# The low halves of the GLU's weights: VectorE behind the last scan in place of GpSimd, nine parts loaded ahead, and the GLU begun on high halves

## The chip, the cores and the metric

The kernel runs on one core of one Trainium2 chip. The metric is the time of one execution in device microseconds (us). Three executions of the kernel before gave 2034.98, 2035.56 and 2037.89 us; the median is 2035.56 us. One further execution was recorded by the hardware profiler; all times of single instructions come from it, counted from the start of its span.

## The reference: what is computed

One layer of an encoder: an S5 state-space mixer with a gated linear unit (GLU), then a convolutional feed-forward network (FFN), over 2048 tokens of width 1024 and 16 tokens put ahead of them. Cut to what matters here:

```
u  = (rms_norm(h) @ w_in).reshape(b, L, 64 groups, 16)
s  = associative scan over time of  s[t] = a * s[t-1] + B u[t]     (complex, 64 states a group)
y  = gelu(Re(C s) + d * u)                                         (b, L, 1024)
a, g = split(y @ w_glu, 2)                                         (w_glu is 1024 x 2048)
h  = h + a * sigmoid(g)
h  = h + conv_ffn(rms_norm(h))
```

## The kernel before

**Products in halves.** Every large matrix product is made of float16 halves. A float32 operand is scaled, rounded to float16 (the high half), and what rounding lost is kept as a second float16 (the low half). A product is the sum of three matmuls: high by high, high by low, low by high. For the GLU the weights' halves are `wg[0]` (high) and `wg[1]` (low), the activations' halves are the two planes of `yT`.

**The S5 stage.** The 1024 channels are worked in eight blocks of 128 (`p` or `cb`, 0 to 7). For each block there are: the input product (`emit_u`), tables made by VectorE (`gen_b`, `gen_c`, the latter giving `CA`), a small kernel matrix (`emit_k`, written to DRAM as `kd` and read back in Toeplitz form by `load_toep` as `Toep`), the states' inputs (`emit_v`, giving `S`), a scan in place on VectorE (`scan`, thirty short instructions on `S`, lines 547 to 552), a rearrangement of the scanned states by DMA (`emit_z`: `Z` from `S`), and the output (`emit_y`): 32 tiny matmuls `mp`, then for each of the block's eight groups two matmuls of `U` by `Toep` (L598, L599) and one of `Z` by `CA` (L600); ScalarE's GELU (L602) takes two groups at a time into `yf`, and one DMA (L606) writes `yf` to DRAM as `yd`. In the text y5, y6, y7 and Z6, Z7 and so on are these steps of blocks 5, 6 and 7.

**The GLU's operands.** The weights come in 16 parts (`split_wg`, part i holds rows 128*(i//2) of the weight and one half of its 2048 columns): GpSimd issues the load of 512 KB into a staging tile `gst` (L96); then the part is split. In the kernel before, parts 0 to 7 are split by two ScalarE operations (L102 scales in place, L103 rounds to `wg[0]`) and one of GpSimd (L104 subtracts, giving `wg[1]`); parts 8 to 15 by two of VectorE (L99, L100). As a part is split, the next one's load is issued. The activations come in 16 tiles of 128 tokens: `load_y` reads columns of `yd` (SyncE, L113), `prep_y` makes the halves `yh` (L123 or L125 the high one, L126 the low one), and SyncE issues two transposing DMAs (L128) into `yT`. A tile may be taken in pieces: columns of blocks 0 to 4, 5 and 6, 7 for tile 0; 0 to 6 and 7 for tile 1. A tile needs 8 (blocks) x 3 (half products) x 4 (quarters of the columns) = 96 matmuls (`glu_mm`, L137); tiles 0 and 1 together 192.

**Order.** Every engine and queue runs its instructions in the order in which the program lists them; nothing is rescheduled (`manual_schedule`). A DMA is listed on the queue of the engine that issues it, and that queue stands still while its next instruction waits. The last two blocks are written out by hand at the end of the S5 stage. Block 6's pass (`pen`) interleaves its scan with block 7's tables and the first `prep_y` of tile 0; then, outside the loop, come `gen_c(7)`, `emit_k(7)`, the scan of block 7, `emit_y(6)`, `emit_z(7)`, the first GLU matmuls of tile 0, the loads of tile 1 and of blocks 5 and 6 of tile 0, `emit_y(7)`, and the rest. After that only TensorE's work is left for the GLU: the remaining matmuls of tiles 0 and 1, tiles 2 to 15, and then the FFN.

Of the kernel before, what the change touches and what calls it, by code (L numbers as in the profile page):

```python
# [44 lines left out]
def tile_kernel(ctx: ExitStack, tc: tile.TileContext, x, meta, norm_mix, norm_ffn, w_in, lam_re, lam_im, log_dt,  # L45
# [45 lines left out]
    def split_wg(i, pool, tag, bufs):  # L91

        dk, hh = divmod(i, 2)
        cs_ = slice(D * hh, D * hh + D)
        st = pool.tile([P, D], F32, tag=tag, bufs=bufs, name=f"gst{dk}_{hh}")
        PO.dma_start(out=st, in_=w_glu[0, dk * P:(dk + 1) * P, cs_])  # L96
        yield
        if wg_eng[0] is V:
            V.tensor_scalar(wg[0][:, dk, cs_], st, GS, None, op0=ALU.mult)  # L99
            V.scalar_tensor_tensor(wg[1][:, dk, cs_], st, GS, wg[0][:, dk, cs_], op0=ALU.mult, op1=ALU.subtract)  # L100
        else:
            A.activation(st, st, AF.Copy, scale=GS)  # L102
            A.copy(wg[0][:, dk, cs_], st)  # L103
            PO.tensor_tensor(wg[1][:, dk, cs_], st, wg[0][:, dk, cs_], op=ALU.subtract)  # L104
# [10 lines left out]
    def prep_y(t, tile_of, d0=0, d1=DK, eng=A):  # L115

        w = P * (d1 - d0)
        if t not in yT:
            yT[t] = gl.tile([P, 2, DK, P], F16, tag="yT", bufs=2, name=f"yT_{t}")
        yt = yts.pop(t)  # L120
        yh = [tile_of("yh", [P, D], F16, f"yh{t}_{d0}_{i}") for i in range(2)]
        if eng is A:
            A.activation(yh[0][:, 0:w], yt[:, 0:w], AF.Copy, scale=YS)  # L123
        else:
            V.tensor_scalar(yh[0][:, 0:w], yt[:, 0:w], YS, None, op0=ALU.mult)  # L125
        V.scalar_tensor_tensor(yh[1][:, 0:w], yt[:, 0:w], YS, yh[0][:, 0:w], op0=ALU.mult, op1=ALU.subtract)  # L126
        for i in range(2):
            SY.dma_start_transpose(out=yT[t][:, i, d0:d1], in_=yh[i][:, 0:w])  # L128

    def glu_mm(t, d0=0, d1=DK):  # L130
        if t not in gps:
            tags = ("u", "u", "v", "v") if t % 2 == 0 else ("t", "t", "y", "y")
            gps[t] = [psum.tile([P, 512], F32, tag=tags[i], name=f"g{t}_{i}") for i in range(4)]
        for dk in range(d0, d1):
            for (a, b) in ((0, 0), (0, 1), (1, 0)):
                for o in range(4):
                    PE.matmul(out=gps[t][o], lhsT=yT[t][:, a, dk], rhs=wg[b][:, dk, 512 * o:512 * o + 512],  # L137
                              start=(dk == 0 and a + b == 0), stop=(dk == DK - 1 and a == 1))


    with ExitStack() as c2:
# [437 lines left out]
        def emit_y(cb, mid=None):  # L579
# [14 lines left out]
            for gp in range(4):  # L594
# [8 lines left out]
                             yp.rearrange("p g (t h) -> p g t h", h=T), AF.Gelu_apprx_tanh)  # L603
                if mid:
                    mid(gp)
            PO.dma_start(out=yd[0:T, :, cb * P:(cb + 1) * P].rearrange("t k c -> k t c"),  # L606
                         in_=yf.rearrange("p t g h -> p t (g h)"))

        def drive(*gens):
            gens = list(gens)  # L610
# [99 lines left out]
            return s5.tile(shape, dt, tag=tag, bufs=bufs, name=nm)  # L710

        def wg_load(i):
            wgs.append(split_wg(i, *((s5, "wit", 2) if i in (6, 7, 11, 12) else (ld, "win", 3))))
            next(wgs[i])

        def wg_split(i0, i1, eng=PO):
            for i in range(i0, i1):
                wg_eng[0] = eng
                next(wgs[i], 0)
                if len(wgs) < 16:  # L720
                    wg_load(len(wgs))

        for p in range(NCB - 1):
            take = quads[:takes[p]]
# [3 lines left out]
            def uq(i, dks=range(DK)):  # L728
                if i < len(take):
                    emit_u(*take[i], dks=dks)  # L730
                    if DK - 1 in dks:
                        evict_u(*take[i])
# [58 lines left out]

    hc2 = ctx.enter_context(tc.tile_pool(name="hc2", bufs=1, side="right"))
# [661 lines left out]
```

## Time and profile before

| | |
|---|---|
| median of three executions | 2035.56 us |
| the profiled execution, its own time | 2040.73 us |
| its span, first to last instruction | 2038.9 us |
| TensorE busy over the span, instructions | 1923.3 us (94%), 10992 |
| VectorE busy | 1384.9 us (68%) |
| ScalarE busy | 645.2 us (32%) |
| GpSimd busy | 577.2 us (28%) |
| mean granted TensorE clock | 0.979 |

A row of the timeline gives start, duration (both us), engine, line, operation, output and inputs by the program's names, shapes and count; in square brackets stands how long the engine was idle just before it and what ended that. PE is TensorE, DVE is VectorE, ACT is ScalarE, POOL is GpSimd, SP is SyncE; a `q` behind the name is the engine's queue as it issues DMAs. A row of the windows gives a stretch of the span, its length, each engine's busy time with the number of its instructions in brackets, the clock granted to TensorE (1.00 is full speed), the DMA engines' busy share and what they moved in GB/s. In rows about one tile, three durations are minimum/median/maximum in ns.

### The profile page before, as it was taken

How to read it: one execution, taken by the hardware profiler on the slowest of the kernel's cores; microseconds unless marked ns; L12 is line 12 of the kernel's file. 1: busy time of each engine (PE TensorE's matmuls, PEld its weight loads, DVE VectorE, ACT ScalarE, POOL GpSimd, SP SyncE). 2: the span in 40 equal slices, each digit the busy share in tenths (PEclk: the TensorE clock that was granted, in tenths of full speed). 3: DMA queues.
4: the chain of work that ended last, by engine and by line, in shares of the span. 5: the costliest groups of instructions: out<-in, count | busy, mean ns of one | idle time of the engine just before them, and what ended most of it. 6: DMA issues, size and time to landing. Idle time of an engine off the chain costs nothing.

```text
span 2038.9 us, 28973 instructions
## 1 busy us (share of the span) xinstructions
PE 1923.3 (94%) x10992; PEld 957.5 (47%) x10992; DVE 1384.9 (68%) x1709; ACT 645.2 (32%) x1057; POOL 577.2 (28%) x644
## 2 busy tenths in 40 slices
PE   3699999689999999999999989999999999999999
PEld 3456666445444444444444434334444444444444
DVE  3489999944444348999999961345466666668982
ACT  5433423312222224544445441222222232322110
POOL 4221212400000014555555500366000001117630
PEclk9799999789999999999999999999999999999999
DMA  9967766958566656444444489999533333336443
GB/s 187 188 136 140 176 138 150 229 139 185 130 140 158 147 150 178 143 156 148 146 157 148 151 243 274 310 324 303 171 104 101 102 104 101 101 99 156 144 124 93
DMA packets 337223, 329.92 MB, mean 162 GB/s; under 512 B 150700, under 2 KB 238332, under 8 KB 337084
## 3 DMA queue, kind: packets, MB, share of 16 engines
q1 hardware_dynamic: 319164, 286.01, 52.9%
q0 software_dynamic: 8496, 27.30, 4.7%
q10 hardware_dynamic: 9424, 14.76, 2.9%
q8 instruction: 86, 1.41, 0.3%
q14 instruction: 53, 0.43, 0.1%
HBM read 183.82 MB, written 108.45 MB: 143 GB/s over the span
## 4 chain that ended last, share of the span: by engine, by line
PE 66%; DVE 8%; DMA 4%; issue 2%; ACT 1%; POOL 1%; SPq 1%; DVEq 0%; ACTq 0%; POOLq 0%
PE g L137 15%; PE p L78 11%; PE p L76 11%; PE p L77 11%; PE pq L76 3%; PE pq L77 3%; PE pq L78 3%; PE po L76 2%; PE po L77 2%; PE po L78 2%; DMA wc<-wcd 1%; DMA wcd<-wc 1%; DVE wc L914 1%; DVE y L1132 1%; DVE y L1131 1%
## 5 line engine op out<-in xcount | busy, mean ns | idle before, releaser
L76 PE MATMUL p<-hc,wc 128*128 128x512 f16 x1232 | 467.3, 379 | 2.3 <-DMA hc<-hl 1.7
L78 PE MATMUL p<-hc,wc 128*128 128x512 f16 x1232 | 467.5, 379 | 1.7 <-DVE wc L914 1.7
L77 PE MATMUL p<-hc,wc 128*128 128x512 f16 x1232 | 467.4, 379 | 0.9 <-DMA hc<-hl 0.9
L137 PE MATMUL g<-wg,yT 128*128 128x512 f16 x1536 | 334.3, 381 | 0.7 <-DMA yT<-yh 0.7
L914 DVE SCALAR_TENSOR_TENSOR wc<-fst,wc 128x512 f16<-128x512 f32 x209 | 184.7, 892 | 109.9 <-ACT wc L908 91.4
L137 PEld LDWEIGHTS <-yT 128*128 128x128 f16 x1536 | 150.2, 98 | 183.1 <-issue 2.6
L908 ACT ACTIVATE wc<-fst 128x512 f16<-128x512 f32 x209 | 125.9, 625 | 229.6 <-POOL fst L873 97.5
L78 PEld LDWEIGHTS <-wc 128*128 128x128 f16 x1232 | 120.2, 98 | 148.7 <-DVE wc L914 3.8
L76 PEld LDWEIGHTS <-wc 128*128 128x128 f16 x1232 | 120.1, 98 | 140.0 <-issue 1.8
L77 PEld LDWEIGHTS <-wc 128*128 128x128 f16 x1232 | 120.2, 98 | 138.9 <-DMA hc<-hl 1.2
L76 PE MATMUL pq<-wc,act 128*128 128x512 f16 x352 | 135.2, 384 | 16.6 <-DMA wc<-wcd 11.1
L76 PE MATMUL u<-hnT,win 128*128 128x512 f16 (+2 forms) x352 | 115.2, 337 | 25.6 <-DMA hnT<-hl 14.8
L77 PE MATMUL pq<-wc,act 128*128 128x512 f16 x352 | 135.1, 384 | 0.0
L78 PE MATMUL pq<-wc,act 128*128 128x512 f16 x352 | 134.8, 383 | 0.0
L77 PE MATMUL u<-hnT,win 128*128 128x512 f16 (+2 forms) x352 | 114.9, 337 | 16.9 <-DMA hnT<-hl 16.9
L76 PE MATMUL po<-wc,act 128*128 128x512 f16 x308 | 117.6, 382 | 3.4 <-DVE res L1292 3.4
L77 PE MATMUL po<-wc,act 128*128 128x512 f16 x308 | 117.6, 382 | 0.0
L78 PE MATMUL po<-wc,act 128*128 128x512 f16 x308 | 117.4, 381 | 0.0
L78 PE MATMUL u<-hnT,win 128*128 128x512 f16 (+2 forms) x352 | 115.0, 337 | 0.0
L1123 ACT ACTIVATE act<-hu,cwt 128x1024 f32<-128x1024 f32 x44 | 54.6, 1241 | 185.6 <-DVE hu L1224 141.3
L77 PEld LDWEIGHTS <-act 128*128 128x128 f16 x660 | 64.8, 98 | 99.1 <-issue 23.3
L1123 ACT ACTIVATE y<-hu,cwt 128x1024 f32<-128x1024 f32 x44 | 54.6, 1240 | 162.3 <-DVE hu L1224 123.2
(328 smaller groups left out, 2983.6 us busy)
## 6 DMA issues: line engine op xcount, KB each, us to landing
wc<-wcd SPq DMA_DIRECT2D x275, 256.0 KB, 2.7
wcd<-wc SPq DMA_DIRECT2D x253, 256.0 KB, 3.2
fst<-in_ffn_w_up_dram SPq DMA_DIRECT2D x44, 512.0 KB, 5.1
fst<-in_ffn_w_down_dram SPq DMA_DIRECT2D x44, 512.0 KB, 5.8
ud<-us SPq DMA_DIRECT2D x32, 258.0 KB, 5.3
U<-ud SPq DMA_DIRECT2D x16, 516.0 KB, 3.5
Toep<-kd SPq DMA_DIRECT2D x64, 128.0 KB, 5.4
yd<-yf POOLq DMA_DIRECT2D x8, 1024.0 KB, 7.6
```

The costliest lines, as they stand in the source:

```text
L76: PE.matmul(out=ps, lhsT=sh, rhs=mh, start=first, stop=False)
L77: PE.matmul(out=ps, lhsT=sh, rhs=ml, start=False, stop=False)
L78: PE.matmul(out=ps, lhsT=sl, rhs=mh, start=False, stop=last)
L137: PE.matmul(out=gps[t][o], lhsT=yT[t][:, a, dk], rhs=wg[b][:, dk, 512 * o:512 * o + 512], start=(dk == 0 and a + b == 0), stop=(dk == DK - ...
L908: A.activation(w[:, 0], src, AF.Copy, scale=GS)
L914: V.scalar_tensor_tensor(w[:, 1], src, GS, w[:, 0], op0=ALU.mult, op1=ALU.subtract)
L1123: A.activation(y, hu[:, 2:18], AF.Identity, bias=cwt[:, 3, c:c + 1], scale=cwt[:, 2, c:c + 1])
L1131: V.scalar_tensor_tensor(y, hu[:, 1:17], cwt[:, 1, c:c + 1], y, op0=ALU.mult, op1=ALU.add)
L1132: V.scalar_tensor_tensor(y, hu[:, 0:16], cwt[:, 0, c:c + 1], y, op0=ALU.mult, op1=ALU.add)
```

## The change

What it does, by steps:

- GpSimd's subtraction (L104) and VectorE's pair (L99, L100) are gone. All 16 parts take the same way: ScalarE scales in place and rounds (`wg_hi`), and VectorE makes the low half by one TENSOR_TENSOR (`wg_lo`, L101 of the changed file).
- All 16 of these VectorE operations stand behind the last instruction of block 7's scan. No low half is made before.
- Nine parts have a staging place of their own ahead of any low half. Parts 0 to 2 are loaded as before; 3 to 5 behind `transp(7)`; 6 to 8 behind `gen_c(7)`, into the places of tables that nobody reads any more. Part i + 9 is loaded when part i's low half is made.
- The high half of tile 0's pieces and of tile 1's first piece (`prep_y`) is made by ScalarE in place of VectorE; VectorE still makes the low one.
- The GLU of tile 0 begins with the products that need the weights' high halves alone: blocks 0 and 1 ahead of `emit_k(7)`, blocks 2 and 3 behind `emit_y(6)`. Their products with the low halves (`los`) stand directly ahead of `emit_y(7)`. The kernel before had done 12 + 24 = 36 GLU matmuls ahead of `emit_y(7)`, the changed one has 48 there.
- `emit_z(7)` stands behind `load_y` of tile 1 and of blocks 5 and 6 of tile 0; before, it stood ahead of them.
- The DMAs that write `yd` of blocks 6 and 7 are issued by SyncE in place of GpSimd.

```diff
-        if wg_eng[0] is V:
-            V.tensor_scalar(wg[0][:, dk, cs_], st, GS, None, op0=ALU.mult)
-            V.scalar_tensor_tensor(wg[1][:, dk, cs_], st, GS, wg[0][:, dk, cs_], op0=ALU.mult, op1=ALU.subtract)
-        else:
-            A.activation(st, st, AF.Copy, scale=GS)
-            A.copy(wg[0][:, dk, cs_], st)
-            PO.tensor_tensor(wg[1][:, dk, cs_], st, wg[0][:, dk, cs_], op=ALU.subtract)
+        A.activation(st, st, AF.Copy, scale=GS)
+        A.copy(wg[0][:, dk, cs_], st)
+        yield
+        V.tensor_tensor(wg[1][:, dk, cs_], st, wg[0][:, dk, cs_], op=ALU.subtract)
+        yield
...
-            for (a, b) in ((0, 0), (0, 1), (1, 0)):
+            for (a, b) in of:
...
-            PO.dma_start(out=yd[0:T, :, cb * P:(cb + 1) * P].rearrange("t k c -> k t c"),
-                         in_=yf.rearrange("p t g h -> p t (g h)"))
+            (PO if cb < NCB - 2 else SY).dma_start(out=yd[0:T, :, cb * P:(cb + 1) * P].rearrange("t k c -> k t c"),
+                                                   in_=yf.rearrange("p t g h -> p t (g h)"))
...
+            slots = [(ld, "win", 3)] * 3 + [(s5, "wit", 2)] * 2 + [(ld, "wst", 1), (s5, "tmp", 1), (s5, "pre", 1), (s5, "pim", 1)]
+            wgs.append(split_wg(i, *slots[i % 9]))
...
+        def wg_lo(i0, i1):
+            for i in range(i0, i1):
+                next(wgs[i])
+                if i + 9 < 2 * DK:
+                    wg_load(i + 9)
...
-                fills.append(prep_y(0, s5_tile, 0, NY[0], V) for _ in range(1))
+                fills.append(prep_y(0, s5_tile, 0, NY[0]) for _ in range(1))
...
         p = NCB - 1
-        wg_split(3, 4)
-        wg_load(7)
-        wg_load(8)
+        his, los = ((0, 0), (1, 0)), ((0, 1),)
+        wg_hi(3, 6)
         drive(gen_c(p))
-        glu_mm(0, 0, 1)
+        for i in range(6, 9):
+            wg_load(i)
+        glu_mm(0, 0, 2, his)
         emit_k(p)
         load_toep(p)
-        wg_split(4, 6)
         drive(scan(p))
-        emit_y(p - 1, lambda gp: wg_split(6 + gp, 7 + gp - gp // 2))
-        emit_z(p)
-        glu_mm(0, 1, 3)
+        emit_y(p - 1)
+        wg_hi(6, 8)
+        glu_mm(0, 2, 4, his)
         load_y(1, s5_tile, 0, NY[1])
         load_y(0, s5_tile, NY[0], NY[1])
-        wg_split(8, 12, V)
-        emit_y(p)
-        glu_mm(0, 3, NY[0])
-        prep_y(1, s5_tile, 0, NY[1], V)
-        prep_y(0, s5_tile, NY[0], NY[1], V)
-        wg_split(12, 16, V)
+        emit_z(p)
+        wg_lo(0, 2)
+        prep_y(0, s5_tile, NY[0], NY[1])
+        prep_y(1, s5_tile, 0, NY[1])
+        wg_lo(2, 8)
+        wg_hi(8, 9)
+        glu_mm(0, 0, 4, los)
+        emit_y(p, lambda gp: wg_hi(9 + gp, 10 + gp))
+        wg_lo(8, 13)
+        glu_mm(0, 4, NY[0])
+        wg_hi(13, 16)
+        wg_lo(13, 16)
```

Where instructions move, at three places. In the rows below stand line, operation, output and inputs with the program's numbers, and shape. (The changed file's lines are two less than before's in this part.)

SyncE's queue around Z7, in the kernel before (`kd1` and `Toep7` are block 7's kernel matrix, `yt1_0` the columns of blocks 0 to 6 of tile 1, `yt0_5` those of blocks 5 and 6 of tile 0):

```order
L515 DMA kd1_106<-ks7_3798 32x1x256 x4
L522 DMA Toep7_3804<-kd1_106 16x8x256 x8
L575 DMA Z7_3927<-S7_3710 64x4x128 x4
L113 DMA yt1_0_3956<-yd_69 128x896
L113 DMA yt0_5_3958<-yd_69 128x256
```

The same place in the changed kernel (`yf6` is y6's result, `yh0_5` the halves of `yt0_5`):

```order
L513 DMA kd1_106<-ks7_3802 32x1x256 x4
L520 DMA Toep7_3808<-kd1_106 16x8x256 x8
L604 DMA yd_69<-yf6_3877 128x16x128
L111 DMA yt1_0_3931<-yd_69 128x896
L111 DMA yt0_5_3933<-yd_69 128x256
L573 DMA Z7_3935<-S7_3707 64x4x128 x4
L126 DMA_TRANSPOSE yT_0_3600<-yh0_5_0_3946 128x2x128
```

The store of y6 has come onto this queue, and Z7 has moved from ahead of the two loads to behind them; the loads read what that store writes.

VectorE behind the last instruction of block 7's scan, in the kernel before (`gst4_0` and `gst4_1` are parts 8 and 9):

```order
L552 TENSOR_TENSOR S7_3710<-S7_3710,stab7d0_3859 128x8x63
L99 TENSOR_SCALAR wg0_3489<-gst4_0_3754 128x1024
L100 SCALAR_TENSOR_TENSOR wg1_3490<-gst4_0_3754,wg0_3489 128x1024
L99 TENSOR_SCALAR wg0_3489<-gst4_1_3816 128x1024
L100 SCALAR_TENSOR_TENSOR wg1_3490<-gst4_1_3816,wg0_3489 128x1024
```

The same place in the changed kernel (`gst0_0`, `gst0_1`, `gst1_0`, `gst1_1` are parts 0 to 3):

```order
L550 TENSOR_TENSOR S7_3707<-S7_3707,stab7d0_3853 128x8x63
L101 TENSOR_TENSOR wg1_3490<-gst0_0_3491,wg0_3489 128x1024
L101 TENSOR_TENSOR wg1_3490<-gst0_1_3493,wg0_3489 128x1024
L124 SCALAR_TENSOR_TENSOR yh0_5_1_3947<-yt0_5_3933,yh0_5_0_3946 128x256
L124 SCALAR_TENSOR_TENSOR yh1_0_1_3954<-yt1_0_3931,yh1_0_0_3953 128x896
L101 TENSOR_TENSOR wg1_3490<-gst1_0_3495,wg0_3489 128x1024
L101 TENSOR_TENSOR wg1_3490<-gst1_1_3701,wg0_3489 128x1024
```

Two low halves come first, then the low halves of the two activation pieces, then the other low halves of the weights.

VectorE in block 6's scan, where the first piece of tile 0 is split, in the kernel before:

```order
L547 TENSOR_TENSOR stab6k0_3607<-S6_3398,asc_101 128x16x15
L125 TENSOR_SCALAR yh0_0_0_3610<-yt0_0_3497 128x640
L126 SCALAR_TENSOR_TENSOR yh0_0_1_3611<-yt0_0_3497,yh0_0_0_3610 128x640
L550 TENSOR_TENSOR S6_3398<-S6_3398,stab6k0_3607 128x8x15
L552 TENSOR_TENSOR S6_3398<-S6_3398,stab6k0_3607 128x8x15
```

The same place in the changed kernel:

```order
L545 TENSOR_TENSOR stab6k0_3598<-S6_3398,asc_101 128x16x15
L124 SCALAR_TENSOR_TENSOR yh0_0_1_3602<-yt0_0_3497,yh0_0_0_3601 128x640
L548 TENSOR_TENSOR S6_3398<-S6_3398,stab6k0_3598 128x8x15
L550 TENSOR_TENSOR S6_3398<-S6_3398,stab6k0_3598 128x8x15
L545 TENSOR_TENSOR stab6k1_3609<-S6_3398,asc_101 128x16x14
```

The high half `yh0_0_0` is no longer made here: it has gone to ScalarE, behind the four GELUs of y5 and the high halves of parts 0 to 2, and VectorE's low half, with the rest of block 6's scan behind it, reads it.

More of the change, by code (lines that the diff above doesn't have):

```diff
@@ L85, in tile_kernel @@
     gl = cl.enter_context(tc.tile_pool(name="gl", bufs=1))
-    wg, yT, gps, wg_eng = [], {}, {}, [PO]
+    wg, yT, gps = [], {}, {}
     def alloc_wg():
@@ L128, in prep_y, with glu_mm @@
             SY.dma_start_transpose(out=yT[t][:, i, d0:d1], in_=yh[i][:, 0:w])
-    def glu_mm(t, d0=0, d1=DK):
+    def glu_mm(t, d0=0, d1=DK, of=((0, 0), (0, 1), (1, 0))):
         if t not in gps:
@@ L183, in tile_kernel @@
         NG = NCB * G
-        pre = s5.tile([P, NG, T + 1], F32, name="pre")
-        pim = s5.tile([P, NG, T + 1], F32, name="pim")
+        pre = s5.tile([P, NG, T + 1], F32, tag="pre", name="pre")
+        pim = s5.tile([P, NG, T + 1], F32, tag="pim", name="pim")
         coef = s5.tile([P, NCB, 4, G], F32, name="coef")
@@ L712, in wg_load, with wg_hi @@
         def wg_load(i):
-            wgs.append(split_wg(i, *((s5, "wit", 2) if i in (6, 7, 11, 12) else (ld, "win", 3))))
+            slots = [(ld, "win", 3)] * 3 + [(s5, "wit", 2)] * 2 + [(ld, "wst", 1), (s5, "tmp", 1), (s5, "pre", 1), (s5, "pim", 1)]
+            wgs.append(split_wg(i, *slots[i % 9]))
             next(wgs[i])
-        def wg_split(i0, i1, eng=PO):
+        def wg_hi(i0, i1):
             for i in range(i0, i1):
[L718 to L721, printed above, removed]
+                next(wgs[i])
+        def wg_lo(i0, i1):
+            for i in range(i0, i1):
+                next(wgs[i])
+                if i + 9 < 2 * DK:
+                    wg_load(i + 9)
         for p in range(NCB - 1):
@@ L745, in tile_kernel @@
             if p:
-                emit_y(p - 1, (lambda gp: wg_split(gp, gp + (gp < 3))) if pen else None)
+                emit_y(p - 1, (lambda gp: wg_hi(gp, min(3, gp + 1))) if pen else None)
             if pen:
-                fills.append(prep_y(0, s5_tile, 0, NY[0], V) for _ in range(1))
+                fills.append(prep_y(0, s5_tile, 0, NY[0]) for _ in range(1))
             fills = itertools.chain(*fills)
@@ L762, in tile_kernel @@
             transp(p + 1)
+            if pen:
+                for i in range(3, 6):
+                    wg_load(i)
             uq(2, range(0, 4))
@@ L769, in tile_kernel @@
         p = NCB - 1
-        wg_split(3, 4)
-        wg_load(7)
-        wg_load(8)
+        his, los = ((0, 0), (1, 0)), ((0, 1),)
+        wg_hi(3, 6)
         drive(gen_c(p))
-        glu_mm(0, 0, 1)
+        for i in range(6, 9):
+            wg_load(i)
+        glu_mm(0, 0, 2, his)
         emit_k(p)
         load_toep(p)
-        wg_split(4, 6)
         drive(scan(p))
-        emit_y(p - 1, lambda gp: wg_split(6 + gp, 7 + gp - gp // 2))
-        emit_z(p)
-        glu_mm(0, 1, 3)
+        emit_y(p - 1)
+        wg_hi(6, 8)
+        glu_mm(0, 2, 4, his)
         load_y(1, s5_tile, 0, NY[1])
         load_y(0, s5_tile, NY[0], NY[1])
-        wg_split(8, 12, V)
-        emit_y(p)
-        glu_mm(0, 3, NY[0])
-        prep_y(1, s5_tile, 0, NY[1], V)
-        prep_y(0, s5_tile, NY[0], NY[1], V)
-        wg_split(12, 16, V)
+        emit_z(p)
[10 more added lines that the diff above has]
+        wg_lo(13, 16)
     hc2 = ctx.enter_context(tc.tile_pool(name="hc2", bufs=1, side="right"))
```

## The prediction

> **What bounds the kernel now.** I read the page first, then the windows, TensorE's timeline, and those of VectorE, ScalarE and SyncE. The windows show the only stretch after the start where TensorE is starved, the end of the S5 stage:
>
> ```profile
> 370.00:380.00 10.00, 3.13 (x26) 1.36 (x23) 9.86 (x9) 1.91 (x2) 3.67 (x4) 0.72 1.04 238
> 400.00:410.00 10.00, 4.08 (x49) 2.13 (x47) 9.48 (x17) 0.17 (x1) 0.50 (x1) 0.93 0.71 220
> 430.00:440.00 10.00, 10.00 (x48) 4.57 (x47) 0.56 (x2) 0.31 (x1) 1.58 (x3) 1.00 0.70 205
> ```
>
> TensorE is busy 3.13 and 4.08 of 10 us there while VectorE is busy 9.86 and 9.48; from 430 on TensorE is full at clock 1.00. TensorE's waits in that stretch:
>
> ```profile
> 382.19 1.08 PE L504 MATMUL kp<-CA,bb 128*32 128x256 f32 x8 [2.48 <-DVE CA L493]
> 384.65 0.61 PE L588 MATMUL mp<-U,Toep 128*32 128x1 f32 x32 [1.30 <-DMA Toep<-kd]
> 387.25 1.19 PE L600 MATMUL yp<-CA,Z 128*128 128x256 f32 x2 [0.41 <-DMA Z<-S]
> 397.45 5.34 PE L137 MATMUL g<-wg,yT 128*128 128x512 f16 x24
> 412.26 1.22 PE L600 MATMUL yp<-CA,Z 128*128 128x256 f32 x2 [7.93 <-DMA Z<-S]
> 424.38 33.83 PE L137 MATMUL g<-wg,yT 128*128 128x512 f16 x156
> 458.92 41.61 PE L137 MATMUL g<-wg,yT 128*128 128x512 f16 x192 [0.71 <-DMA yT<-yh]
> ```
>
> From 424.38 TensorE runs without a hole to the end of tiles 0 and 1 (156 matmuls in 33.83 us, 0.217 each), and tile 2 begins at 458.92. What follows is TensorE's own work, which the change leaves alone. So what the change is worth is read at one point: when does y7 end, and how many of the 192 matmuls are then left. Before that stands Z7, which waits for block 7's scan, and VectorE is that scan's engine:
>
> ```profile
> 353.92 2.38 DVE L125 TENSOR_SCALAR yh<-yt 128x640 f16<-128x640 f32 x1
> 357.23 2.70 DVE L550 TENSOR_TENSOR S<-S,stab6k 128x120 f32<-128x120 f32 x1
> 360.38 2.68 DVE L547 TENSOR_TENSOR stab6k<-S,asc 128x224 f32<-128x224 f32 x1
> 372.08 2.60 DVE L552 TENSOR_TENSOR S<-S,stab6d 128x504 f32<-128x504 f32 x1
> 385.89 0.63 DVE L550 TENSOR_TENSOR S<-S,stab7u 128x256 f32<-128x256 f32 x1
> 386.56 2.37 DVE L552 TENSOR_TENSOR S<-S,stab7u 128x256 f32<-128x256 f32 x1
> 388.96 2.91 DVE L547 TENSOR_TENSOR stab7u<-S,asc 128x256 f32<-128x256 f32 x1
> 392.76 0.59 DVE L547 TENSOR_TENSOR stab7k<-S,asc 128x240 f32<-128x240 f32 x1
> 393.39 2.29 DVE L550 TENSOR_TENSOR S<-S,stab7k 128x120 f32<-128x120 f32 x1
> 395.71 0.38 DVE L552 TENSOR_TENSOR S<-S,stab7k 128x120 f32<-128x120 f32 x1
> 396.12 2.68 DVE L547 TENSOR_TENSOR stab7k<-S,asc 128x224 f32<-128x224 f32 x1
> 407.69 0.69 DVE L552 TENSOR_TENSOR S<-S,stab7d 128x504 f32<-128x504 f32 x1
> L104 POOL TENSOR_TENSOR wg<-gst,wg x8: 2113/2140/2577, 353.4 to 396.3; 128x1024 f16<-128x1024 f32 x8
> ```
>
> Instructions of one size take 0.38 or 2.29, 0.59 or 2.68, 0.69 or 2.60 us. There are eight long ones, and eight GpSimd subtractions of 2.14 us.
>
> **Removing GpSimd's subtractions.** With the short rows as measure, the scan of block 6 loses 2.70-0.38, 2.68-0.59 and 2.60-0.69, together 6.3 us; the scan of block 7 loses 2.37-0.63, 2.91-0.63, 2.29-0.38 and 2.68-0.59, together 8.0. The eighth, at 353.92, goes with its instruction. I take all of it as won.
>
> **The high half on ScalarE.** Part of it is given back at once. VectorE reaches the low half of tile 0's first piece at 353.92, and must now wait for ScalarE, whose y5 work is queued ahead:
>
> ```profile
> 358.24 0.59 ACT L602 ACTIVATE yf<-yp 128x512 f32<-128x512 f32 x1
> L123 ACT ACTIVATE yh<-yt x16: 309/1052/1057, 434.1 to 704.8; 128x1024 f16<-128x1024 f32 x14, 128x128 f16<-128x128 f32 x2
> 357.66 2.92 SPq L128 DMA_TRANSPOSE yT<-yh x2
> ```
>
> The last GELU ends at 358.8; a 640-wide rounding lies between 0.31 (128) and 1.05 (1024), some 0.7; so the low half starts near 359.6 and the scan goes on at 360.3 instead of 357.23: 3.1 us late. Net, block 6's scan and `gen_c(7)` end 3.2 us early, and the kernel matrix of block 7 is done near 380 (382.19+1.2-3.2). Block 7's scan ends 3.2+8.0 = 11.2 us early: 408.4-11.2 = 397.2. On SyncE the first transposition can start at 359.5, the second 1.46 later, so the pair ends at 362.4 instead of 360.6: `kd` of block 6, `Toep6` and Z6, queued behind it, are issued 1.8 us later.
>
> **y6.** It ran from Z6's arrival at 387.25 to 397.45, 10.2 us. Its matrix `kp` is ready earlier, but it waited for `Toep6` and Z6 last, which are now issued 1.8 us later; against that, three weight loads that went out beside them come after `gen_c(7)`. Bounds: 1.8 us later, if the transfers take as long as before; 4 us earlier, if only `kp` held it back and both arrive by 383. I leave it where it was, nearest to the rows that show it waiting for DMA twice.
>
> **The SyncE queue.** This is the term that decides. Ahead of Z7 now stand y6's store and two loads that read what it writes:
>
> ```profile
> 397.65 0.60 ACT L602 ACTIVATE yf<-yp 128x512 f32<-128x512 f32 x1 [1.23 <-PE yp L600]
> DMA to landing us min/median/max: 8.8/8.8/8.8
> DMA to landing us min/median/max: 6.1/7.6/9.8
> 408.44 2.66 SPq L575 DMA_DIRECT2D Z<-S  x4
> 411.19 1.03 SPq L113 DMA_DIRECT2D yt<-yd  x2
> 416.85 0.63 DVE L125 TENSOR_SCALAR yh<-yt 128x896 f16<-128x896 f32 x1 [1.03 <-DMA yt<-yd]
> yt<-yd SPq DMA_DIRECT2D x2, 64.0 KB, 1.9
> ```
>
> y6's last GELU ends at 398.25. The store (8.8 us for that of y6, the first landing row; 6.1 to 9.8 over all eight, the second) lands at 407.1 when issued at 398.3; the loads are issued by 408.1; Z7 goes out then, against 408.44 before. So the scan's 11.2 us do not reach Z7. The store goes from GpSimd's queue to SyncE's, which no row shows for it; I take y6's own 8.8, and 6.1 and 9.8 as ends. The second load lands 1.9 us (64 KB) to 5.6 us (416.85 less 411.19, behind a full DMA) after issue; I take 2.5 for its 128 KB. Call that landing M: 410.6, with ends from 403 (early y6, quick store and load) to 417.
>
> The Trainium skill, "DMA: Bandwidth & Descriptors", section "Anatomy of one DMA — SWDGE (gpsimd) path", fits a transfer as 2.0 us plus its bytes over 436 GB/s: an estimate of 4.4 us for this 1 MB. No landing of `yd` in this trace comes under 6.1; by the page the sum below would be 4.4 us smaller, still a loss.
>
> **VectorE behind M.** Two low halves are made by 399.5 and then VectorE stands, with the other fourteen queued, until the tile pieces come:
>
> ```profile
> 409.01 1.23 DVE L100 SCALAR_TENSOR_TENSOR wg<-gst,wg 128x1024 f16<-128x1024 f32 x1
> 417.51 6.23 SPq L128 DMA_TRANSPOSE yT<-yh x4
> 417.52 1.09 DVE L126 SCALAR_TENSOR_TENSOR yh<-yt,yh 128x896 f16<-128x896 f32 x1
> 421.95 0.43 DVE L126 SCALAR_TENSOR_TENSOR yh<-yt,yh 128x256 f16<-128x256 f32 x1 [0.69 <-DMA yT<-yh]
> ```
>
> There are two `yh` buffers, so the second piece waits until the first's transposes have landed. In order: ScalarE's half 0.4, then the first transposition at M+0.5, the second 1.25 later at M+1.75, landing 3.1 after its start as at 421.95 (second issue about 418.8): M+4.9; the 896-wide low half, 1.09: M+6.0; six low halves of parts 2 to 7 at about 1.15 (rows of 1.23, overlapping): M+12.9. Only then can TensorE finish `los`, which stand ahead of y7: y7 starts at M+13.5.
>
> **y7.** TensorE has then been nearly idle since about 402, and y5 shows what a start after idling costs:
>
> ```profile
> 346.29 0.70 PE L598 MATMUL yp<-Toep,U 128*128 128x256 f32 x2
> 350.43 0.65 PE L598 MATMUL yp<-Toep,U 128*128 128x256 f32 x2
> 352.66 0.59 PE L598 MATMUL yp<-Toep,U 128*128 128x256 f32 x2
> ```
>
> Two groups take 4.14 us at first, the next two 2.23. Eight groups at 1.1 and 0.4 for `mp` make 9.2, and the slow start 1.9: y7 ends at M+24.6. By the Trainium skill, "TensorE: Matmul & The Clock Gate", section "What's actually happening", some 3.4 us pass at half rate after an idle window, an estimate of 1.7 us lost in place of 1.9; the trace bears it out, and the sum would be 0.2 smaller.
>
> **Behind y7.** 144 matmuls are left (192-48), 31.2 us. ScalarE makes parts 9 to 15 between and behind y7's GELUs, two operations each of about the 1.05 of the L123 row; part 13 comes just as block 6 of tile 0 wants it, and I charge 1.0 us. Tiles 0 and 1 end at M+56.8 = 467.4, before at 458.2: 9.2 us lost. The wait of 0.71 ahead of tile 2 stays, since `yT` has two places and TensorE frees the one it needs.
>
> **The rest.** The new staging places, loads 3 to 8 and the high halves of parts 0 to 8 cost nothing, as ScalarE idles through 400 to 410 (0.17 busy); without that cover each part would cost 2.1.
>
> **The sum.** +9.2 on the profiled execution, whose own 2040.73 is 5.2 above the median of 2035.56. I put the difference on the median, a little less because a quicker execution has quicker transfers: 2044.5.
>
> **The rivals.**
> *The scan's gain comes through (faster).* If the store and the two loads land before the scan's end, VectorE never waits, and y7 starts at 399.5+13.5. That is M at 399.5, 11.1 earlier: 1.9 us gained, 3.8 with a warm clock. It decides at a store issued before 388; for it speaks that VectorE alone bounded the old stretch, against it that y6 did not even begin before 384.65 and waited on DMA then. A gain over 4.1 us would need y6 some 12 us earlier as well: 0.07, mostly for a dependency that I have read wrong.
> *Transfers land quickly (no measurable change).* y6 2 us early, the store in 6.1, the load in 1.9: M 405.3, 5.3 earlier, +3.9; at the lowest ends of all, about +1.7. The DMA engines are fuller before (1.04 at 370 to 380) than they will be with loads 6 to 8 moved back. 0.20.
> *The tail of the weights also stalls (slower still).* Parts 11 to 15 are loaded only as low halves 2 to 6 are made, all behind M; if they land late, or the last piece of tiles 0 and 1 comes after TensorE wants it, 2 to 5 us are added: +11 to +14. 0.15.
> *The long VectorE instructions are not GpSimd's doing.* Then the scan ends at 405.2, still ahead of M: nothing changes in the sum.
>
> **Chances.** The forecast itself has 0.58. Plus or minus 0.2%, 4.1 us, is about what a measurement of this kernel can tell from no change. Faster 0.07, same 0.20, slower 0.73 (0.58+0.15). The range takes M from 402.5 to 415, which is +1 to +13.5: 2036 to 2049.
>
> **What would show it.** Right: no VectorE instruction of either scan over 1.4 us; VectorE idle about 5.5 us ahead of the low half of tile 0's first piece, waiting for ScalarE; scan 7 ending near 397; Z7 issued near 408, behind a SyncE wait for the store; a VectorE wait of about 10 us behind the second low half; y7 starting near 424 and ending near 435. Wrong: Z7 issued right behind the scan, or y7 starting before 415.

## The result and the profile after

The changed kernel takes 2045.39 us, the median of 11 executions (2041.33 to 2052.45); the kernel before, run beside it, 2035.56 us. The ratio is 1.0058 with a 95% interval of 1.0043 to 1.0074, which is 8.8 to 15.1 us, 11.8 in the middle. The forecast of 9 us lost lies in that interval, near its lower end; the way there was wrong in its first half, ahead of y6, and mostly right in its second.

The profiled execution has a span of 2048.3 us, 9.4 more than before. That difference has three parts. Up to the end of y5 this execution was 7.6 us earlier: y5's last GELU ends at 351.24 in place of 358.83, out of the first 100 us, in which TensorE's waits for the input differ (it is busy for 56.3 us of them in this execution, 48.9 before). Between the end of y5 and the start of tile 2 it lost 12.8 us, and behind tile 2, 4.2 us. So below the stretch from the end of y5's last GELU to the start of tile 2 is the measure, in three pieces. ScalarE's last GELU of y5, of y6 and of y7 in the changed kernel:

```profile
350.65 0.59 ACT L600 ACTIVATE yf<-yp 128x512 f32<-128x512 f32 x1
...
397.08 0.60 ACT L600 ACTIVATE yf<-yp 128x512 f32<-128x512 f32 x1 [1.58 <-PE yp L598]
...
432.65 0.59 ACT L600 ACTIVATE yf<-yp 128x512 f32<-128x512 f32 x1
```

Together with TensorE's rows of the same stretch:

```profile
385.37 0.61 PE L586 MATMUL mp<-U,Toep 128*32 128x1 f32 x32 [13.49 <-DMA Z<-S]
...
416.04 5.36 PE L135 MATMUL g<-wg,yT 128*128 128x512 f16 x10 [11.94 <-DVE wg L101]
...
422.24 0.43 PE L586 MATMUL mp<-U,Toep 128*32 128x1 f32 x32
...
464.12 41.61 PE L135 MATMUL g<-wg,yT 128*128 128x512 f16 x192 [0.75 <-DMA yT<-yh]
```

TensorE now stands for 13.49 us ahead of y6, for the transfers `Toep6` and Z6, and 11.94 us ahead of `los`, for VectorE's low halves; y7 begins right behind `los`. From the end of y5 to the end of y6 are 46.4 us (39.4 before), from there to the end of y7 35.6 (26.9 before), from there to tile 2 30.9 (33.7 before, when 12 more matmuls were left).

VectorE's rows are of the kind that the prediction said they would be:

```profile
351.95 0.83 DVE L124 SCALAR_TENSOR_TENSOR yh<-yt,yh 128x640 f16<-128x640 f32 x1 [5.25 <-issue]
...
389.10 2.35 DVE L101 TENSOR_TENSOR wg<-gst,wg 128x1024 f16<-128x1024 f32 x2
410.04 0.43 DVE L124 SCALAR_TENSOR_TENSOR yh<-yt,yh 128x256 f16<-128x256 f32 x1 [18.59 <-ACT yh L121]
413.76 1.09 DVE L124 SCALAR_TENSOR_TENSOR yh<-yt,yh 128x896 f16<-128x896 f32 x1 [3.30 <-DMA yT<-yh]
414.77 8.03 DVE L101 TENSOR_TENSOR wg<-gst,wg 128x1024 f16<-128x1024 f32 x7
```

The scan ends at 389.1 and two low halves are made; then VectorE stands idle for 18.59 us with the other low halves queued behind a tile piece that has not been loaded. SyncE's queue shows why y6, and with it that piece, came late:

```profile
355.07 4.73 SPq L513 DMA_DIRECT2D kd<-ks  x4
369.33 5.81 SPq L520 DMA_DIRECT2D Toep<-kd  x8
375.27 6.55 SPq L573 DMA_DIRECT2D Z<-S  x4
...
397.70 0.40 SPq L604 DMA_DIRECT2D yd<-yf  x1
405.25 0.80 SPq L111 DMA_DIRECT2D yt<-yd  x2
406.16 2.72 SPq L573 DMA_DIRECT2D Z<-S  x4
```

And of its waits, those for `kd` (total in us, times, longest; the longest is the one for `kd6`):

```profile
SPq L520 <- DMA kd<-ks: 10.8, 3, 9.4
```

`kd6` is issued by 359.8, and `Toep6`, which reads it, only at 369.33: SyncE waited 9.4 us at a stretch for it to land. The same two rows of the kernel before, where that wait was 6.3 us:

```profile
360.68 2.73 SPq L515 DMA_DIRECT2D kd<-ks  x4
369.86 5.51 SPq L522 DMA_DIRECT2D Toep<-kd  x8
```

Counted from the end of y5, `Toep6` goes out 18.1 us behind it in place of 11.0. Of these 7.1 us, 2.0 lie ahead of `kd6` (its first issue comes 3.8 us behind y5 in place of 1.9, behind the transposes that wait for ScalarE's high half), 2.0 in its four issues (4.73 us in place of 2.73) and 3.1 in the wait for its landing. What else was on its way, GpSimd's queue tells; first that of the kernel before, then of the changed one:

```profile
363.01 0.56 POOL L96 DMA_DIRECT2D gst<-in_s_w_glu_dram  x1 [0.30 <-POOL wg L104]
363.57 1.19 POOL L606 DMA_DIRECT2D yd<-yf  x1
```

```profile
352.25 1.18 POOL L604 DMA_DIRECT2D yd<-yf  x1 [16.11 <-ACT cs L473]
353.79 0.54 POOL L96 DMA_DIRECT2D gst<-in_s_w_glu_dram  x1 [0.36 <-PE wt L463]
355.12 1.06 POOL L96 DMA_DIRECT2D gst<-in_s_w_glu_dram  x2 [0.79 <-PE wt L463]
```

Before, GpSimd's subtractions held its queue, and y5's store of 1 MB went out at 363.57, 4.7 us behind y5's end and behind `kd6` (issued 360.68 to 363.4). Freed of them, GpSimd sends it 1.0 us behind y5's end, and three weight loads of 512 KB with it, all ahead of or beside `kd6`. Three such loads went out around `kd6` in the kernel before, too, at 356.96, 360.00 and 363.01, spaced by the subtractions; the store ahead of `kd6` is what is new.

### The profile page after: what moved, and what is told of

Its sections match the earlier page's. It is cut to its first block, busy times and chain, and to the rows that moved or that the text cites. A ratio compares the mean times of both kernels' runs of the same rounds, so it can differ in the third digit from the quotient of the medians.

```text
span 2048.3 us, 28979 instructions
## 1 busy us (share of the span) xinstructions
PE 1925.1 (94%) x10992; PEld 956.4 (47%) x10992; DVE 1369.9 (67%) x1706; ACT 663.3 (32%) x1076; POOL 561.6 (27%) x634
## 4 chain that ended last, share of the span: by engine, by line
PE 74%; DMA 9%; DVE 7%; ACT 3%; issue 3%; SPq 3%; POOL 1%; ACTq 0%; DVEq 0%; POOLq 0%
PE g L135 14%; PE p L78 12%; PE p L76 12%; PE p L77 12%; PE pq L76 3%; PE pq L77 3%; PE pq L78 3%; PE po L76 2%; PE po L77 2%; PE po L78 2%; DMA hnT<-hl 1%; PE u L77 1%; PE u L76 1%; PE u L78 1%; DMA wc<-wcd 1%
## 5 line engine op out<-in xcount | busy, mean ns | idle before, releaser
L135 PE MATMUL g<-wg,yT 128*128 128x512 f16 x1536 | 341.1, 384 | 21.1 <-DVE wg L101 12.5
L77 PEld LDWEIGHTS <-act 128*128 128x128 f16 x660 | 65.0, 98 | 99.4 <-issue 23.8
```

The source lines that it names most:

```text
L77: PE.matmul(out=ps, lhsT=sh, rhs=ml, start=False, stop=False)
```

## The experiments

Two theories stand against each other. **The order theory**: the time is lost in two places, ahead of y6 (bulk transfers in front of `kd6`) and between y6 and y7 (low halves that VectorE makes behind the tile pieces, with `los` ahead of y7). **The queue theory**: SyncE's queue decides, since Z7 stands behind y6's store. The prediction brings in its deciding term in this way, though its sum then runs over the landing of the loads and VectorE's low halves. Behind them is the question whether taking the subtractions from GpSimd was worth anything. Each run was compared with the kernel before on its own chip; the times are differences of marks in one profiled execution each. Where an expectation counts from y5's last GELU it means that instruction's start, 0.6 us ahead of the end used in the table.

| run | y5 to y6 | y6 to y7 | y7 to tile 2 | sum | ratio to before (95%) |
|---|---|---|---|---|---|
| before | 39.4 | 26.9 | 33.7 | 100.1 | 1 |
| changed | 46.4 | 35.6 | 30.9 | 112.9 | 1.0058 (1.0043 to 1.0074) |
| a_z_first | 47.7 | 34.3 | 30.9 | 112.9 | 1.0063 (1.0050 to 1.0076) |
| n_los_behind | 45.0 | 28.4 | 34.0 | 107.3 | 1.0027 (1.0009 to 1.0044) |
| b_lows_first | 46.1 | 33.0 | 30.9 | 109.9 | 1.0039 (1.0020 to 1.0057) |
| g_no_flood | 45.0 | 28.6 | 30.9 | 104.4 | 1.0025 (1.0012 to 1.0038) |
| d_kd6_clear | 40.8 | 37.1 | 30.9 | 108.7 | 1.0039 (1.0024 to 1.0055) |
| j_y6_early | 37.4 | 36.1 | 30.9 | 104.4 | 1.0024 (1.0010 to 1.0038) |
| e_gpsimd_lows | 41.1 | 38.4 | 30.9 | 110.4 | 1.0032 (1.0020 to 1.0044) |
| p_store_gpsimd | | | | | 1.0068 (1.0050 to 1.0087) |
| l_two_edits | 37.0 | 28.4 | 30.9 | 96.2 | 0.9975 (0.9963 to 0.9988) |
| h_y7_free | 45.4 | 19.5 | 36.4 | 101.3 | 1.0022 (1.0007 to 1.0037) |
| i_all | 37.2 | 22.7 | 34.9 | 94.8 | 0.9990 (0.9977 to 1.0003) |
| k_best | 37.7 | 22.2 | 36.6 | 96.5 | 0.9988 (0.9975 to 1.0001) |

Where a row has a sum, the sum less 100.1 agrees with the ratio less 1, times 2035.56, to within 4 us.

**Z7 ahead of the loads (a_z_first).**

```
+        emit_z(p)
         load_y(1, s5_tile, 0, NY[1])
         load_y(0, s5_tile, NY[0], NY[1])
-        emit_z(p)
```

> One edit on the changed kernel: block 7's Z goes ahead of the two loads of yt on SyncE, so no longer behind y6's store. Theory (y7 is held by the low halves that VectorE makes behind the tile pieces, not by Z7): Z7 goes out near 393, right behind Toep7, but y7 still starts 12 to 13 us behind the landing of the second yt load, near 422; the time stays within 3 us of the changed kernel's 2045.4. Rival (SyncE's queue decides, since Z7 stands behind the store): y7 starts by 406 and the time falls by 10 us or more, to 2035 or less.

SyncE's queue of this run, and TensorE's wait:

```profile
399.18 0.40 SPq L604 DMA_DIRECT2D yd<-yf  x1
399.70 5.36 SPq L573 DMA_DIRECT2D Z<-S  x4
406.06 0.81 SPq L111 DMA_DIRECT2D yt<-yd  x2
...
416.29 4.04 PE L135 MATMUL g<-wg,yT 128*128 128x512 f16 x8 [9.29 <-DVE wg L101]
```

Z7 goes out 6.5 us earlier, and nothing follows from it: TensorE waits for low halves until 416.29, and the ratio is that of the changed kernel. The queue theory fails: Z7's place in the queue decides nothing here. The expectation had one number wrong, 393: Z7 stands behind the store of y6 here too, and the code gives it the place of Z6 (one buffer), which y6 reads to its end.

**`los` behind y7 (n_los_behind).**

```
-        glu_mm(0, 0, 4, los)
         emit_y(p, lambda gp: wg_hi(9 + gp, 10 + gp))
+        glu_mm(0, 0, 4, los)
```

> One edit on the changed kernel: the sixteen low-half products of blocks 0 to 3 of tile 0 stand behind y7 on TensorE instead of ahead of it; VectorE's and SyncE's order stay. Theory (y7 was ready from the landing of Z7, about 4 us behind its issue, and waited 12 us only for the six low halves that VectorE makes behind the tile pieces): y7's last GELU ends 25 to 28 us behind y6's (35.6 in the changed kernel), tile 2 starts 58 to 62 us behind y6's (67.0), the ratio to the kernel before is 1.001 to 1.004. Rival (y7 is held by the tile pieces or ScalarE's order as well): y7's last GELU still ends 32 us or more behind y6's, ratio 1.005 or above.

Nearly as expected (25 to 28): y7 ends 28.4 us behind y6 in place of 35.6. Of the 7.2 us won, 3.1 are given back behind y7, where the 16 matmuls of `los` now stand (16 x 0.217 = 3.5). The net of 4 us, and 1.4 by which y6 came sooner in this execution, make the sum of 107.3; the ratio agrees.

**All low halves first (b_lows_first), and the same without its transfers (g_no_flood).**

```
-        wg_lo(0, 2)
+        wg_lo(0, 8)
         prep_y(0, s5_tile, NY[0], NY[1])
         prep_y(1, s5_tile, 0, NY[1])
-        wg_lo(2, 8)
```

> One edit on the changed kernel: all eight low halves of parts 0 to 7 stand on VectorE ahead of the tile pieces instead of two. Theory: the eight are made by about 399 (389 + 8 x 1.2), so y7 starts when Z7 lands, about 4 us behind its issue at 406, near 411 in place of 422; the end of tiles 0 and 1 comes 5 to 11 us earlier, less whatever the seven weight loads cost that now go out beside y6's store (up to 6 us on its landing): 2034 to 2041. Rival (the loss sits in y6's lateness or in the tail of the weights): y7 starts earlier but the time stays at 2043 or more.

As a low half is made, its place is loaded with the part nine further on. The store of y6 and the loads that read it, in this run:

```profile
393.94 0.40 SPq L604 DMA_DIRECT2D yd<-yf  x1
407.82 0.80 SPq L111 DMA_DIRECT2D yt<-yd  x2
408.73 2.69 SPq L573 DMA_DIRECT2D Z<-S  x4
```

13.9 us from store to loads, in place of 7.5: seven loads of 512 KB went out between 387.3 and 398.0. TensorE's wait for the low halves is gone, but Z7 is late in its stead, and only 2.6 us remain of the gain ahead of y7's end. The second run has only parts 9 and 10 loaded at once, and 11 to 15 by SyncE behind the first piece's transposes:

```
-                if i + 9 < 2 * DK:
+                if i < 2:
                     wg_load(i + 9)
...
         prep_y(0, s5_tile, NY[0], NY[1])
+        for i in range(11, 16):
+            wg_load(i)
         prep_y(1, s5_tile, 0, NY[1])
```

> The run with all eight low halves ahead of the tile pieces once more, but of the seven weight loads that they release only parts 9 and 10 go out at once; 11 to 15 stand on SyncE behind the transposes of the first piece. Theory (in that run the seven loads of 512 KB held y6's store: 13.9 us from issue to the next load, in place of 7.5): the store takes 7 to 9 us again, y7's last GELU ends 25 to 28 us behind y6's (35.6 in the changed kernel, 33.0 in that run) and the ratio to the kernel before is 1.001 to 1.003. Rival (the weights' tail binds): parts 11 to 15, now later, stall TensorE behind y7 for 5 us or more and the ratio stays at 1.004 or above.

```profile
392.17 0.40 SPq L604 DMA_DIRECT2D yd<-yf  x1
400.18 0.80 SPq L111 DMA_DIRECT2D yt<-yd  x2
```

8.0 us again, y7 ends 28.6 behind y6 (25 to 28 expected), and the later loads stall nothing behind y7. The flood was the cause of the 13.9 us, and the second place costs 7 us by the order of VectorE's work and of the loads.

**y5's store behind Z6 (d_kd6_clear).**

```
             emit_z(p)
             transp(p + 1)
             if pen:
-                for i in range(3, 6):
-                    wg_load(i)
+                store_y(p - 1)
+                wg_load(3)
```

The store (`store_y`) is taken out of `emit_y(5)` and listed on SyncE behind Z6. Loads 4 and 5 were listed behind `gen_c(7)` as well, which did nothing: GpSimd's queue does not wait for VectorE there, and they went out with load 3. So the run is of the store alone.

> One edit on the changed kernel: the store of y5 (1 MB) goes on SyncE behind Z6, and weight loads 4 and 5 with 6 to 8, so that kd6 no longer shares the DMA engines with them (of the four, load 3 stays). Theory (kd6 landed 9.4 us behind its last issue since the store of y5 and three weight loads went out ahead of it): Toep6 is issued near 363 in place of 369, y6 starts near 378 in place of 385, and all behind it comes 6 to 8 us earlier: 2037 to 2040. Rival (y6 is tied to the transfers' own time or to other work): Toep6 still waits 6 us or more, y6 starts near 385, the time stays within 2 us of 2045.4.

```profile
347.17 2.58 SPq L514 DMA_DIRECT2D kd<-ks  x4
356.55 5.08 SPq L521 DMA_DIRECT2D Toep<-kd  x8
361.75 3.07 SPq L574 DMA_DIRECT2D Z<-S  x4
365.29 0.40 SPq L610 DMA_DIRECT2D yd<-yf  x1
...
377.06 1.08 ACT L601 ACTIVATE yf<-yp 128x512 f32<-128x512 f32 x2 [7.19 <-DMA yd<-yf]
```

`Toep6` is issued 12.7 us behind y5's end in place of 18.1, and y6 begins 23.8 us behind it in place of 34.1. But its GELUs then wait 7.19 us: `yf` has one buffer, and y5's late store was still reading it. 5.7 us of the 10 remain, where 6 to 8 were expected. With the store gone, `kd6`'s four issues take 2.58 us again and the wait for its landing is 6.7 us, near the 2.73 and 6.3 of the kernel before.

**y5's store between `kd6` and `Toep6` (j_y6_early).** And loads 4 and 5 on SyncE behind Z6.

```
             emit_k(p)
+            if pen:
+                store_y(p - 1)
             uq(1)
             load_toep(p)
```

> On the changed kernel, y6's supply alone: y5's store is issued on SyncE directly behind kd6 (so kd6 goes first, and the store early enough to free yf), and weight loads 4 and 5 on SyncE behind Z6. Theory (what delayed y6 is bulk in front of kd6): y6's last GELU ends 37 to 40 us behind y5's (46.4 in the changed kernel, 39.4 in the one before, 40.8 with the store behind Z6), nothing behind y6 changes, and the ratio to the kernel before is 1.001 to 1.003 (1.0058 for the changed kernel). Rival (Toep6 and Z6 now meet the store instead): 43 us or more, ratio 1.004 or above.

```profile
349.33 2.52 SPq L514 DMA_DIRECT2D kd<-ks  x4
351.90 0.59 SPq L610 DMA_DIRECT2D yd<-yf  x1
355.59 5.08 SPq L521 DMA_DIRECT2D Toep<-kd  x8
```

SyncE now waits 3.0 us for `kd6` to land, `Toep6` goes out 9.6 us behind y5's end, and y6 ends 37.4 behind it: 9 us won, 2 more than the change had lost. Nothing behind y6 moved.

**GpSimd's low halves back (e_gpsimd_lows).** Parts 0 to 7 are subtracted by GpSimd right behind their high halves, and VectorE makes none of these.

```
         A.copy(wg[0][:, dk, cs_], st)
+        if i < 8:
+            PO.tensor_tensor(wg[1][:, dk, cs_], st, wg[0][:, dk, cs_], op=ALU.subtract)
         yield
-        V.tensor_tensor(wg[1][:, dk, cs_], st, wg[0][:, dk, cs_], op=ALU.subtract)
+        if i >= 8:
+            V.tensor_tensor(wg[1][:, dk, cs_], st, wg[0][:, dk, cs_], op=ALU.subtract)
```

> One part of the change undone: GpSimd makes the low halves of parts 0 to 7 again, directly behind their high halves; VectorE makes only those of 8 to 15. Theory (the eight subtractions cost VectorE time in the scans that nothing waits for, while low halves behind the tile pieces hold y7): VectorE has instructions of over 2 us again beside each subtraction, scan 7 ends some 5 us later than 389, and yet y7 starts when Z7 lands, near 411 in place of 422, and the time falls by 6 to 11 us: 2034 to 2039. Rival (a quick scan is worth its time): the scan's lateness passes on, the time stays at 2045 or rises.

Two of VectorE's rows, and GpSimd's queue:

```profile
366.30 3.21 DVE L488 TENSOR_TENSOR CA<-pre,cs 128x1088 f32<-128x1088 f32 x1
369.44 3.20 DVE L491 TENSOR_TENSOR ctm<-pim,cs 128x1088 f32<-128x1088 f32 x1
```

```profile
339.61 10.45 POOL L101 TENSOR_TENSOR wg<-gst,wg 128x1024 f16<-128x1024 f32 x3 [6.86 <-ACT wg L99]
350.00 1.21 POOL L607 DMA_DIRECT2D yd<-yf  x1
```

The same two instructions in the changed kernel:

```profile
363.61 1.28 DVE L485 TENSOR_TENSOR CA<-pre,cs 128x1088 f32<-128x1088 f32 x1
364.81 1.28 DVE L488 TENSOR_TENSOR ctm<-pim,cs 128x1088 f32<-128x1088 f32 x1
```

The long instructions are GpSimd's doing: 3.2 us with a subtraction beside them (three more run from 362.56 on), 1.28 without. The Trainium skill, "SBUF — State Buffer", section "SBUF: two separate sides", says that VectorE (with two inputs from SBUF) and GpSimd lock a port pair against each other for a whole instruction; these rows agree. And yet the kernel with the slower scans is faster than the changed one by 5 us. The expected time came, but not by the expected way: y5's store was held behind a subtraction again and left at 350.00, beside `kd6` (349.39 to 351.9), so that y6 came 5.4 us earlier. From y6 to y7 nothing was won (38.4 us): TensorE stood 14.1 us for Z7, issued at 397.28 right behind seven weight loads (393.0 to 396.7). That these loads held it is the reading that b_lows_first suggests; no run here takes them away.

**The stores back on GpSimd (p_store_gpsimd).** Only the issuing engine of y6's and y7's store is undone.

```
-            (PO if cb < NCB - 2 else SY).dma_start(out=yd...
+            PO.dma_start(out=yd...
```

> One part of the change undone: the stores of y6 and y7 are issued by GpSimd again. Theory (the queue hardly matters, what shares the DMA engines does): the loads of yt go out 8 to 10 us behind y6's last GELU (8.2 in the changed kernel), y7 moves by as much, and the ratio stays at 1.005 to 1.008. Rival (SyncE's queue is what delays the store and what stands behind it): Z7 and the loads come earlier, the ratio falls below 1.004.

The ratio says that the queue matters little. The one profiled execution took 7092.71 us: TensorE worked without a stop, but its matmuls began some 0.8 us apart in place of 0.217, so its times are not in the table. The loads behind y6's store went out 7.1 us behind its issue there (7.5 in the changed kernel).

**The two edits together (l_two_edits)**: j_y6_early and g_no_flood.

> The two smallest edits that each gained, together on the changed kernel: y5's store behind kd6 with loads 4 and 5 behind Z6, and the eight low halves first with parts 11 to 15 loaded behind the first piece. Theory (one delay lies ahead of y6, the other between y6 and y7, so they add: tile 2 started 113.5 us behind y5's last GELU in the changed kernel and 105.0 in each of the two): tile 2 starts 96 to 99 us behind y5's last GELU (100.7 in the kernel before), the ratio is 0.997 to 1.000. Rival (they share a cause): 103 or more, ratio 1.002 or above.

TensorE from y7's end on, and SyncE's rows of y6's store and the loads behind it:

```profile
407.25 6.64 PE L135 MATMUL g<-wg,yT 128*128 128x512 f16 x30
...
439.63 41.70 PE L135 MATMUL g<-wg,yT 128*128 128x512 f16 x192 [0.76 <-DMA yT<-yh]
```

```profile
380.40 0.38 SPq L610 DMA_DIRECT2D yd<-yf  x1
385.56 0.81 SPq L111 DMA_DIRECT2D yt<-yd  x2
```

The gains add: 112.9 less 8.5 less 8.5 would be 95.9, and the sum is 96.2. The ratio 0.9975 is 5 us below the kernel before, 17 below the changed one: the change's own pieces in another order, with y5's store and some of the loads on SyncE, are faster than both.

**y7 freed further (h_y7_free, i_all, k_best).** In the first, Z7 has a place of its own (that of the scan's tables) and stands ahead of y6's store, y7 is written where `Toep6` was, `los` stand behind y7, and tile 1's blocks 0 to 4 go ahead of tile 0's 5 and 6. The second adds j_y6_early. The third has y7's store on SyncE ahead of parts 14 and 15, and tile 2's load ahead of the last pieces' transposes; its two edits are in the second diff.

```
-            z = s5.tile([P, G, P], F32, tag="Z", name=f"Z{cb}")
+            z = s5.tile([P, G, P], F32, tag="stab" if cb == NCB - 1 else "Z", name=f"Z{cb}")
...
+        emit_z(p)
         emit_y(p - 1)
```

```
+        store_y(p)
+        for i in range(14, 16):
+            wg_load(i)
...
         for t in range(2):
             load_y(t, gp_tile, NY[1], DK)
+        load_y(2, gp_tile)
```

> On the changed kernel, y7 freed of everything but y6: Z7 gets a place of its own and stands on SyncE ahead of y6's store, y7's output goes to the place of Toep6, all eight low halves stand ahead of the tile pieces, the low-half products behind y7, parts 11 to 15 are loaded behind the first piece's transposes, and tile 1's blocks 0 to 4 go ahead of blocks 5 and 6. Theory (VectorE's order and SyncE's order hold y7, 25 us that are nobody's work): Z7 goes out near 393, y7's last GELU ends 16 to 19 us behind y6's (35.6 in the changed kernel), tile 2 starts 50 to 57 us behind y6's last GELU (66.4), and the ratio to the kernel before is 0.998 to 1.001. Rival (the tail of the weights binds instead): TensorE waits over 6 us in all for wg behind y7, and the ratio is 1.002 or above.

> The two edits together: y6's supply cleared and y7 freed. Theory (two separate delays, one ahead of y6 and one between y6 and y7): the gains add, the ratio to the kernel before is 0.993 to 0.998, faster than both kernels. Rival (behind an earlier y7 the weights' parts and the tile pieces bind, so the second gain eats the first): no better than the better one of the two alone, ratio 0.998 or above.

> The run with everything (y6's supply cleared, y7 freed), in which tile 2 then stood 4.2 us waiting: y7's store (13.9 us from the last GELU to the next load, beside five weight loads) and the load of tile 2 behind the last pieces' transposes. Edit: y7's store on SyncE with only parts 11 to 13 loaded ahead of it, and tile 2's load ahead of the last pieces' transposes. Theory: y7's store takes 8 to 10 us, TensorE's wait ahead of tile 2 falls under 1 us, tile 2 starts 90 to 92 us behind y5's last GELU (95.3 in that run, 100.7 in the kernel before), ratio 0.995 to 0.998: faster than both kernels. Rival (parts 14 and 15 come late now, or the rest of the program gives it back): waits for wg of 3 us or more, ratio 0.999 or above.

y7 ends 19.5 to 22.7 us behind y6 (16 to 19 was expected of h_y7_free), but what is won there is partly lost again behind it, and all three missed the ratio that was expected: 1.0022 (0.998 to 1.001), 0.9990 (0.993 to 0.998) and 0.9988 (0.995 to 0.998). Ahead of tile 2, TensorE waits in h_y7_free:

```profile
449.66 40.59 PE L135 MATMUL g<-wg,yT 128*128 128x512 f16 x177 [5.63 <-DVE x L970]
```

The loads that read y7's store go out 14.7 us behind its issue there, 13.9 in i_all and 15.9 in k_best, and 9.4 in the changed kernel. But it is not the store that they wait for last, as two rows of the changed kernel show:

```profile
441.39 1.23 DVE L101 TENSOR_TENSOR wg<-gst,wg 128x1024 f16<-128x1024 f32 x1 [0.81 <-ACT wg L99]
...
442.69 0.80 SPq L111 DMA_DIRECT2D yt<-yd  x2
```

They go out 0.07 us behind the end of VectorE's last low half, in the changed kernel (442.62) and in each of these three runs. In the changed kernel SyncE waits 4.7 us for the store and then 3.9 for VectorE; in k_best 2.0 for the store, 4.6 for weight loads and 3.9 for VectorE. So k_best moved two loads out of the way of a store that was not what came last, and the low half of the first part that it moved then stood 5.48 us for its high half; its three waits for `yT` (3.44, 0.43, 1.59) are no less than the 4.18 of i_all. What holds tile 2 in these runs is by the traces the tail of the low halves; no run varies that tail alone. None of the three is faster than l_two_edits, which leaves y7 later and loses nothing behind it. h_y7_free's ratio is 3 us worse than its sum says; that is within what executions differ by behind tile 2 (1578 to 1589 us to the end of the span) and stays unexplained.

## Why the prediction was right, and where not

**The scans.** Right. No VectorE instruction of either scan is over 1.3 us, the wait ahead of the first piece is 5.25 us (5.5 said), and scan 7 ends at 389.1, 37.9 us behind y5's end; 397.2 against 358.83 was 38.4. e_gpsimd_lows shows that the removed subtractions made the difference, which ends the fourth rival.

**"I leave it where it was" (y6).** This step failed, by 7.0 us: y6 ends 46.4 us behind y5 in place of 39.4. Its bounds, 1.8 us later to 4 earlier, were made from SyncE's queue and from the kernel matrix. About 2 us are the later transposes, which the prediction had worked out as 1.8 and then used as a bound only. The rest is what it left out: an engine relieved of work also issues its DMAs earlier, and y5's store, on GpSimd's queue behind the subtractions, passed `kd6`. d_kd6_clear moves the store alone and gets 5.7 us back; j_y6_early moves it and two loads and gets 9.0.

**"This is the term that decides" (the SyncE queue).** Half right. The tile pieces do hang on y6's store and its loads: M, the landing of the second load, comes 11.9 us behind y6's end (12.4 said; the loads are issued 7.5 us behind the store, 8.8 was taken). Z7's place in that queue decides nothing, as a_z_first shows; what y7 waits for is the next step.

**VectorE behind M.** Right: M is at 409.6, the first low half of the six at 414.8, y7 starts 12.7 us behind M (13.5 said). n_los_behind and g_no_flood show that this wait, and not VectorE's work, held y7: 7 us in each. The wait itself, behind the second low half, is 18.59 us where about 10 was said, and y7 starts 71.0 us behind y5's end where 65.2 was said: both carry the lateness of y6.

**y7 and what follows.** y7 gives way to the next matmuls 21.8 us behind M (at 431.40), not 24.6. The slow start of 1.9 us was charged because TensorE would come from idling. The slow clock came, but in `los`, which stand ahead of y7: the granted clock is 0.50 from 416 to 421 us and 1.00 from 422 on. There it cost little, for `los` went at VectorE's pace, two matmuls to each low half of 1.15 us: ten in 5.36 us. From 431.40 to the end of tiles 0 and 1 are 32.0 us (31.2 and 1.0 said), the stalls for the weights 0.41.

**The sum.** 7.0 us too little ahead of y6, about 3.5 too much behind it: 12.8 in the profiled stretch, 11.8 by the ratio, 9.2 forecast on the profiled execution. So the number was near by some luck, because two errors partly cancelled, and the sign was safe since both places lose. That a quicker execution has quicker transfers, for which the forecast of 2044.5 took off another 0.3 us, no run here shows. Of the rivals, the scan's gain came through in none of the runs with the changed kernel's order; transfers that land quickly would have needed the reverse of what y6's supply did; the tail of the weights stalled 0.41 us and no more.

**Still open:** whether the change also touches the time ahead of y5's end. Its marks lie at 339.9 to 351.5 us in the twelve profiled executions with the change or a variant of it, at 358.8 in the one before; the ratios fit the sums without any such part, so I take it for a difference between executions.

## What to carry to other kernels

Taking work off an engine also takes the delay off every DMA that it issues; look at what those transfers will now run beside, above all small ones that something waits for. Where an engine idles with work queued, ask which instruction stands ahead of that work and what it waits for: putting six short instructions on the other side of one waiting piece, and holding back the loads that they release, was worth 7 us here; without holding back the loads it was worth 2.6. And a load issued as soon as its buffer is free may cost more than a late one: hold bulk back until the transfer on the path has gone.

## What the runs showed of the hardware

One store, that of y6, of 1 MB from the same queue, lets the loads behind it go after 5.2 us (l_two_edits), 5.8 (j_y6_early), 7.5 (changed), 8.0 (g_no_flood), 9.6 (i_all) or 13.9 (b_lows_first). For the last of these the runs show the reason, seven weight loads issued from 387.3 on, where g_no_flood has two; the smaller differences are not taken apart. The queue that issues it makes no difference that the ratio of p_store_gpsimd shows. The Trainium skill, "DMA: Bandwidth & Descriptors", section "Issuing engines are not separate DMA queues", says that DMAs of all engines end on the same 16 DMA engines and interleave there. The small `kd6`, sent ahead of or beside 2.5 MB of GpSimd's transfers, held SyncE for 9.4 us, for 6.7 with the store taken away (d_kd6_clear), and for 3.0 with the store behind it and two of the loads moved back (j_y6_early): the traces agree, across two queues.
